# Four gathers by depth for each unit of index keys, a tile of its own for block B's keys, and a bit loop of four operations with a slot each

## The chip, the cores and the metric

The kernel runs on one core of a Trainium2 chip. The core has a matrix engine (PE, with its weight load shown apart as PEld), a vector engine (DVE), a scalar engine (ACT) and a general engine (POOL); SP issues most DMA transfers. Each engine works through its own list of instructions in a fixed order and stops at the first one whose inputs, or whose output buffer, are not ready. The metric is the device time of one execution in microseconds (us): lower is better.

## The reference, cut to what matters

The computation is one layer of a decoder for a prompt of 1024 tokens and 8 sequences that each decode 4 tokens over 8192 cached ones.

```python
p = split_proj(rmsnorm(x, norm_in) @ w_in)            # 2048 -> 7760 columns
# sparse attention: an indexer scores every earlier token
ki_past = cache_kidx[page_table].reshape(Bd, past, IDX_DIM)      # 8 x 8192 x 64
ki_all  = jnp.concatenate([ki_past, ki_new], axis=1)
dots = jnp.einsum("bthd,bld->bthl", qi, ki_all)                  # 16 heads x 64
s    = jnp.einsum("bth,bthl->btl", wi, jax.nn.relu(dots))
_, idx = lax.top_k(s, 256)                # 256 kept for each of 8 x 4 queries
phys = page_table[idx // 128]; off = idx % 128
# attention over the gathered rows cache_k[phys, off], cache_v[phys, off]
conv = short_conv(c * h, state, w_conv)                          # width 3
mix  = concat([attn * silu(z_a), b * conv * silu(z_c)])
y    = x + mix @ w_out
```

The prompt goes through the same layer, with its own keys in place of the cache. A page holds 128 tokens.

## The kernel before

**Main stream.** The projections run in two blocks: block A is the first 512 prompt tokens with the 32 decode tokens (matmuls of 288 and 256 columns), block B the last 512 prompt tokens (512 columns). Every product is three matmuls of high and low parts (`pj`, L512). A weight tile `w` comes in over SP's queue, ACT makes its high part `wh` (L494) and DVE its low part `wl`; `w` has 4 buffers, `wl` and `wh` have 3. The order is: block A's indexer queries, `ki`, heads, gates, convolution; then block B's `ki_tile`, `qi_tiles`, `head_tiles(1)`, gates and eight convolution tiles; then `out_proj0` (block A's output, matmuls of `mx` tiles) and `out_proj1`.

**Slots.** After each chunk of four k-tiles (12 matmuls of 512 columns in block B, 24 of 288 and 256 in block A) the code calls `slot()`. In it four "pipes" of generators each go on to their next `yield`: the main pipe (prompt indexer, decode indexer `keys(g, s)`, prompt attention), the `dec` pipe (decode attention, 4 slots of 11), one for the norm, and the vector pipe (selection of the 256 best: `decode_select` calls `decode_find`). A scheduler then sets every engine's order; the slots decide what is near what.

**Decode indexer.** For each of 8 groups of pages and 8 sequences, `keys(g, s)` gathers 128 rows of 2 KB (8 tokens of 64 values) into `G`, transposes it in four PE instructions into the PSUM tile `gt`, makes `gkh` and `gkl` from that, and multiplies (`gd`, `da`). That makes 64 units.

**Decode selection.** `decode_find` ends a search for the threshold, counts with `tot`, gets the shift `doff`, and then packs the kept positions to the left with eight rounds over 2304 int16 values in `S` (one for each bit of the shift). `way` and `ids` turn that into row numbers, PE sums them (`pidx`) and `rid` is the list for the gathers of decode attention. `kt1`, block B's keys, takes over the buffer of `S` (tag "sc").

**Block B's heads.** A projected key tile goes `kraw`, `p` (PE transposes), `kt` and an inverse square root in small steps `kv`, `krh`, `kr`, `krt` on DVE, then `kp` (PE); the indexer's key does the same as `kit` and `kip`.

**End of decode attention.** The outputs `dpo`, `dos`, `dfin` are gated (`dz`) and stored as `doh` and `dol` by 16 small DMAs; only then is "datt" done. Ahead of block B's last convolution tile stands

```python
    while not need <= done:      # "datt" and "at0" to "at3"
        slot()
    conv_tiles(1, 7, x, lambda ch: load_mix(0, range(4 * ch, 4 * ch + 4), x0))
```

`load_mix` issues the 32 loads of the `mxh` and `mxl` tiles (16 k-tiles, high and low), which hold what was stored.

Of the kernel before, what the change touches and what calls it, by code (L numbers as in the profile page):

```python
# [60 lines left out]
def constants():  # L61
    res, dec = Cst(), Cst()
    res.add("ident", np.eye(128))
    r = np.arange(128)
    res.add("tri", np.concatenate([np.zeros((128, 128)), np.where(r[None, :] <= r[:, None], 0.0, NEG)], 1))
    pos_dec = 8192 + np.arange(32) % 4
    rope = np.zeros((128, 9, 48), np.float32)
    for gi in range(9):
        if gi == 4:
            pos = np.concatenate([np.arange(96), pos_dec])  # L70
        else:
            pos = np.arange(128) + 128 * (gi if gi < 4 else gi - 1)
        c, s = _angles(pos, 16)
        rope[:, gi, 0:16], rope[:, gi, 16:32] = c, s
        c, s = _angles(pos, 8)
        rope[:, gi, 32:40], rope[:, gi, 40:48] = c, s
    res.add("rope", rope.reshape(128, -1))
    c, s = _angles(pos_dec, 16)
    res.add("roped", np.concatenate([c, s], 1))
    q = np.arange(32)  # L80
    res.add("newm", np.where(np.arange(4)[None, :] <= (q % 4)[:, None], 0.0, SENT))
    res.add("own", (q[:, None] // 4 == q[None, :] // 4))
    res.add("prow", (r % 16)[:, None])
    wm = np.zeros((128, 8, 2, 32), np.float32)
    for p in range(128):
        for s in range(8):
            wm[p, s, p // 64, s * 4 + (p % 64) // 16] = 1.0
    dec.add("sel8", (np.arange(8)[:, None] == r[None, :] // 16))
    e16 = np.zeros((32, 2, 128), np.float32)
    for qq in range(32):  # L90
        e16[qq, qq // 16, (qq % 16) * 8:(qq % 16) * 8 + 8] = 1.0
    dec.add("e16", e16.reshape(32, -1))
    same = r[:, None] % 32 == r[None, :] % 32
    dec.add("msum", same)
    dec.add("mlow", same & (r[:, None] < r[None, :]))
    selk, selv = np.zeros((128, 132)), np.zeros((128, 2, 32))
    for p in range(128):
        selk[p, p // 8 * 8 + 4 + p % 4] = 1.0
        selv[p, p // 8 % 2, p // 16 * 4 + p % 4] = 1.0
    dec.add("selk", selk)  # L100
    dec.add("selv", selv.reshape(128, -1))
    dec.add("iota", np.broadcast_to(np.arange(256) - 256, (128, 256)))
    dec.add("wmask", wm.reshape(128, -1))
    cq = np.zeros((2, 128, 800), np.float32)
    tok = np.concatenate([np.arange(256, 512), pos_dec, np.arange(512, 1024)])
    c, s = _angles(tok, 8)
    cq[0] = 1.0
    for h in range(2):
        cq[0, h * 64:h * 64 + 8], cq[0, h * 64 + 8:h * 64 + 16] = c.T, c.T
        cq[1, h * 64:h * 64 + 8], cq[1, h * 64 + 8:h * 64 + 16] = -s.T, s.T  # L110
    return res, dec, cq


def build(tc, ctx, I, O, stop=None):
# [40 lines left out]
    def sm(shape, dt=F32, name="sm"):  # L155
        n = int(np.prod(shape[1:]))
        return sp.tile(list(shape), dt, tag="s" if n > 16 else "t", bufs=6 if n > 16 else 16, name=name)
# [4 lines left out]
    def psb(shape=(128, 512), name="psb"):  # L162
        return pp.tile(list(shape), F32, tag="b", bufs=3, name=name)
# [6 lines left out]
    def const(shape, name, dt=F32):  # L170
        return cp.tile(list(shape), dt, name=name, tag=name)
# [64 lines left out]
    def cs(name, rows=128):  # L236
        a, n = res.cols[name]
        return cst[:rows, a - 128:a - 128 + n]
# [38 lines left out]


    hp = [0]
    CY, OS = 1, 2  # L280
    waiting, pipes, later = object(), [], []

    def front(f):
# [201 lines left out]
    def load_w(view, eng=None):  # L485

        m = view.shape[-1]
        with first() if eng is None else nullcontext():
            w = wp.tile([128, 4, 128], F32, tag="w", bufs=4, name="w")
            lo = wp.tile([128, 4, 128], F32R, tag="wl", bufs=3, name="wl")  # L490
            hi = wp.tile([128, 4, 128], F32R, tag="wh", bufs=3, name="wh")
            w, lo, hi = w[:, :, :m], lo[:, :, :m], hi[:, :, :m]
            nc.sync.dma_start(w, view)
            nc.scalar.copy(hi, w)  # L494
            (tt if eng is None else eng.tensor_tensor)(lo, w, hi, SUB)
        return hi, lo
# [214 lines left out]

    def head_tiles(b, x):
        if b == 1:
            while "dsel" not in done:
                slot()
            kt1 = gp.tile([128, 2, 2, 512], F32R, tag="sc", bufs=1, name="kt1")
            kth[1], ktl[1] = kt1[:, 0], kt1[:, 1]
        for kv in range(2):
            follow(k_rest(b, kv, proj1(w_in, C_K + 128 * kv, 128, x, HALVES[b])))
            slot()  # L720
        for kv in range(2):
            follow(v_rest(b, kv, proj1(w_in, C_V + 128 * kv, 128, x, HALVES[b])))
            slot()
        for h in range(8):
            follow(q_rest(b, h, proj1(w_in, C_Q + 128 * h, 128, x, HALVES[b])))
            slot()
        follow(q_norm(b))
# [308 lines left out]
    def decode_index():  # L1036
        while not {"qi0", "ki0"} <= done:
            yield waiting
        st, acc = {}, {}
        cki = I["cache_kidx"].rearrange("o n (r e) d -> (o n r) (e d)", e=8)  # L1040
        zq = lambda z, s: z[:, s].rearrange("p r t h -> p (r t h)")
        keep = dec_c.cols["iota"][0]
        dc = const((128, keep), "dc")
        dcs = lambda k, r=128: dc[:r, dec_c.cols[k][0]:dec_c.cols[k][0] + dec_c.cols[k][1]]
        idx = const((128, 64), "gidx", I32)
        sc["msum"], sc["mlow"] = dcs("msum"), dcs("mlow")
        sc["e16"] = dcs("e16", 32).rearrange("q (g p) -> q g p", g=2)
        sc["selk"], sc["selv"] = dcs("selk"), dcs("selv").rearrange("p (k c) -> p k c", k=2)

        def tables():  # L1050
            nc.sync.dma_start(dc, I["dcst"][:, :keep])
            pt8i, pt8 = sm((8, 64), I32, name="pt8i"), sm((8, 64), name="pt8")
            nc.sync.dma_start(pt8i.rearrange("j (s g) -> j s g", s=8), I["page_table"].rearrange("s (g j) -> j s g", j=8))
            nc.vector.tensor_copy(pt8, pt8i)
            pp8 = psb((128, 64), name="pp8")
            nc.tensor.matmul(pp8, dcs("sel8", 8), pt8, start=True, stop=True)
            ts(idx, pp8, 16.0, cs("prow"), MUL, ADD)
            st["idx"] = idx
            yield 1

# [31 lines left out]
        def keys(g, s):  # L1092
            while "idx" not in st:
                yield 1
            G = g2((128, 512), name="G")
            nc.gpsimd.indirect_dma_start(out=G, out_offset=None, in_=cki,  # L1096
                                         in_offset=bass.IndirectOffsetOnAxis(ap=idx[:, 8 * s + g:8 * s + g + 1], axis=0))
            yield 1
            yield 1
            pt = psb((128, 512), name="gt")  # L1100
            for e in range(4):
                transpose(pt[:, 128 * e:128 * e + 128], G[:, 128 * e:128 * e + 128])
            kh, kl = g2((128, 512), F32R, name="gkh"), g2((128, 512), F32R, name="gkl")
            nc.scalar.copy(kh, pt)
            tt(kl, pt, kh, SUB)
            yield 1
            while "z" not in st:
                yield 1
# [11 lines left out]
            if s == 7:  # L1120
                c = g // 2
                tmp = g2((64, 512), name="stmp")
                nc.scalar.copy(tmp, acc[0][64:128])
                dst = sc["S"][32 * c:32 * c + 32, (g % 2) * 1024:(g % 2) * 1024 + 1024].rearrange(
                    "q (p e r) -> q r e p", e=4, r=2)
                for r in range(2):
                    rs = slice(32 * r, 32 * r + 32)
                    tt(dst[:, r], acc[0][rs].rearrange("q (e p) -> q e p", e=4),
                       tmp[rs].rearrange("q (e p) -> q e p", e=4), ADD)
# [36 lines left out]
    def decode_find():  # L1166
# [54 lines left out]
        for j in range(2):  # L1221
            xj = x[:, 256 + 1024 * j:1280 + 1024 * j]
            stt(xj, mv[:, half[j]], off, eq[j], ADD, MUL)
            ts(xj, xj, -1.0, None, MUL)
            yield 1
        for b in range(8):
            ts(mv, x, 1 << b, None, ALU.bitwise_and)
            ts(mv, mv, 0.0, -1.0, ALU.is_gt, MUL)
            tt(mv, mv, x, ALU.bitwise_and)
            for _ in range(CY):  # L1230
                yield 1
            tt(x, x, mv, ALU.bitwise_xor)
            tt(x[:, :2304 - (1 << b)], x[:, :2304 - (1 << b)], mv[:, 1 << b:], ALU.bitwise_or)
            for _ in range(CY):
                yield 1
        way, ids = g2((128, 256), name="way"), g2((128, 256), name="ids")
        pg, of = (g2((128, 256), I32, name=f"pg{j}") for j in range(2))
        ac, tmp = (g2((128, 256), I16, name=f"pt{j}") for j in range(2))
# [13 lines left out]
        for j in range(1, 16):  # L1252
            ts(tmp, pg, float(j), ptc[:, j:j + 1], ALU.is_equal, MUL)
            tt(ac, ac, tmp, ADD)
            if j % 4 == 3:
                yield 1
        stt(ids, ac, 128.0, of, MUL, ADD)
        stt(ids, way, 0.5, ids, ALU.is_ge, MUL)
# [290 lines left out]
    x = x1  # L1549
# [69 lines left out]
```

## Time and profile before

| | |
|---|---|
| time, median of 3 runs | 2208.34 us (2207.94 to 2208.93) |
| the profiled execution | 2209.53 us |
| its span on the core | 2207.6 us, mean granted clock 0.995 |
| PE busy | 2162.5 us (98%) |
| PEld busy | 1941.8 us (88%) |
| DVE busy | 1317.3 us (60%) |
| ACT busy | 1088.3 us (49%) |
| POOL busy | 480.5 us (22%) |

The span is what the profiler saw between the first and the last instruction; 1.9 us of the execution lie around it. Busy shares are means over stages, so a stage is read from its own rows.

### The profile page before, as it was taken

Reading aid. Unit: us, or ns where it says so; the run is one execution under the profiler, and the core shown is the slowest. Engines: PE = TensorE matmul, PEld = TensorE weight load, DVE = VectorE, ACT = ScalarE, POOL = GpSimd, SP = SyncE. Lnnn points to the kernel's source line nnn. Section 1 sums busy time; section 2 is a strip of 40 time slices with the busy share of each in tenths; the row PEclk is TensorE's granted clock in tenths of the full one; section 3 lists DMA queues with packets and bytes.
Section 4 is the critical chain, followed back from the end, with each engine's and each line's share of the span. In section 5 each row is a group of like instructions: output and inputs, shape, how many; then the busy total and the mean of one; then the engine's idle time right before and its main releaser. Section 6 shows DMA issues by size and latency. Waiting matters only on the chain.

```text
span 2207.6 us, 37829 instructions
## 1 busy us (share of the span) xinstructions
PE 2162.5 (98%) x13502; PEld 1941.8 (88%) x13502; DVE 1317.3 (60%) x2994; ACT 1088.3 (49%) x2112; POOL 480.5 (22%) x697
## 2 busy tenths in 40 slices
PE   6999999999999999999899999999999999999999
PEld 5899999999999999787688888888888899999887
DVE  6556666555555654799866666556667556443222
ACT  4346666334436566422257684445675565332221
POOL 2111011111113222142531143432331111210000
PEclk9999999999999999999999999999999999999999
DMA  5423444344344333333343344433343384448343
GB/s 195 131 90 117 125 138 135 118 141 131 123 144 140 118 116 104 107 117 113 102 134 117 117 150 129 118 122 105 113 128 113 102 301 117 123 119 275 134 134 110
DMA packets 203720, 290.81 MB, mean 132 GB/s; under 512 B 37588, under 2 KB 87948, under 8 KB 203404
## 3 DMA queue, kind: packets, MB, share of 16 engines
q1 hardware_dynamic: 192268, 254.83, 36.0%
q0 software_dynamic: 11264, 33.57, 5.5%
q8 instruction: 106, 1.74, 0.3%
q14 instruction: 82, 0.67, 0.1%
HBM read 247.53 MB, written 40.78 MB: 131 GB/s over the span
## 4 chain that ended last, share of the span: by engine, by line
PE 50%; DMA 0%; DVE 0%; issue 0%; POOL 0%
PE pj L512 33%; PE po L1503 8%; PE ix L855 1%; PE ix L854 1%; PE pt L174 1%; PE lg L1346 1%; PE dpo L1412 1%; PE kst L174 1%; PE sc L178 1%; PE sc L179 1%; PE po L179 1%; PE po L177 1%; PE po L178 1%; PE sc L177 1%; PE p L174 0%; PE pq L174 0%
## 5 line engine op out<-in xcount | busy, mean ns | idle before, releaser
L512 PE MATMUL pj<-xh,wl 128*128 128x288 f32 (+2 forms) x2800 | 793.0, 329 | 6.9 <-DVE wl L121 6.8
L512 PE MATMUL pj<-xh,wh 128*128 128x288 f32 (+2 forms) x2800 | 791.1, 328 | 6.9 <-DVE xl L121 2.7
L512 PE MATMUL pj<-xl,wh 128*128 128x288 f32 (+2 forms) x2800 | 796.1, 330 | 0.0
L121 DVE TENSOR_TENSOR wl<-w,wh 128x512 fp32r<-128x512 f32 (+1 forms) x613 | 444.1, 726 | 431.2 <-ACT wh L494 397.2
L494 ACT CAST wh<-w 128x512 fp32r<-128x512 f32 x616 | 379.2, 616 | 604.8 <-PE pj L512 380.0
L512 PEld LDWEIGHTS pj<-xh,wh 128*128 128x128 f32 (+1 forms) x2800 | 477.1, 189 | 51.8 <-DVE xl L121 3.1
L512 PEld LDWEIGHTS pj<-xh,wl 128*128 128x128 f32 (+1 forms) x2800 | 474.6, 189 | 51.6 <-DVE wl L121 11.2
L512 PEld LDWEIGHTS pj<-xl,wh 128*128 128x128 f32 (+1 forms) x2800 | 475.1, 189 | 42.2
L886 ACT ACTIVATE junk<-acc,se,se 128x512 int8<-128x512 f32 (+5 forms) x186 | 181.1, 974 | 27.4 <-DVE se L121 24.2
L1096 POOL DMA_INDIRECT G<-in_cache_kidx,gidx x64 | 64.3, 1004 | 388.6 <-PE gd L179 140.4
L121 DVE SCALAR_TENSOR_TENSOR acc<-ixr,wsg,acc 128x512 f32<-128x512 f32 (+3 forms) x150 | 98.3, 668 | 45.9 <-ACT ixr L857 44.7
L857 ACT ACTIVATE ixr<-ix,wab 128x512 f32<-128x512 f32 (+3 forms) x160 | 95.3, 613 | 54.9 <-PE ix L855 53.6
L512 PE MATMUL pj<-mxh,wl 128*128 128x272 f32 x512 | 109.8, 292 | 0.0
L512 PE MATMUL pj<-mxl,wh 128*128 128x272 f32 x512 | 109.4, 291 | 0.0
L512 PE MATMUL pj<-mxh,wh 128*128 128x272 f32 x512 | 108.9, 291 | 0.0
L1392 POOL DMA_INDIRECT Vs<-in_cache_v,rid x64 | 66.4, 1038 | 123.8 <-DVE Vl L121 36.1
L1004 ACT CAST pthl<-pt 128x256 fp32r<-128x256 f32 x144 | 49.6, 371 | 80.6 <-PE pt L174 79.4
L121 DVE TENSOR_TENSOR pthl<-pt,pthl 128x256 fp32r<-128x256 f32 x144 | 57.2, 420 | 50.6 <-ACT pthl L1004 50.0
L512 PEld LDWEIGHTS pj<-mxh,wh 128*128 128x128 f32 x512 | 81.5, 189 | 0.7
L512 PEld LDWEIGHTS pj<-mxl,wh 128*128 128x128 f32 x512 | 81.6, 189 | 0.3
L512 PEld LDWEIGHTS pj<-mxh,wl 128*128 128x128 f32 x512 | 81.3, 189 | 0.4
L990 POOL TENSOR_SCALAR P<-P,l 128x128 f32<-128x128 f32 (+7 forms) x64 | 51.9, 811 | 133.5 <-DVE l L989 102.7
(430 smaller groups left out, 3233.7 us busy)
## 6 DMA issues: line engine op xcount, KB each, us to landing
w<-in_w_in SPq DMA_DIRECT2D x480, 256.0 KB
w<-in_w_out SPq DMA_DIRECT2D x128, 256.0 KB
q_d<-qt SPq DMA_DIRECT2D x72, 64.0 KB
xr<-in_x_a SPq DMA_DIRECT2D x16, 272.0 KB
out_y_a<-xr SPq DMA_DIRECT2D x16, 272.0 KB
xq<-in_x_prompt SPq DMA_DIRECT2D x8, 512.0 KB
xq<-in_x_prompt SPq DMA_DIRECT2D x16, 256.0 KB
q<-q_d SPq DMA_DIRECT2D x32, 128.0 KB
```

The lines of the kernel that those rows point to most:

```text
L121: i = f(*a, **k)
L174: nc.tensor.transpose(out, in_, ident[:p, :p])
L177: nc.tensor.matmul(out, lh, rh, start=start, stop=False)
L494: nc.scalar.copy(hi, w)
L512: nc.tensor.matmul(p[:m, :n], w[c][:, k % 4], x[k][b][:, a:a + n], start=(k == 0 and c == b), stop=(k == KT - 1 and c == 1))
L857: nc.scalar.activation(out=r[:, :w], in_=ps[:, :w], func=AF.Relu, scale=wab[:, g, h:h + 1])
L886: nc.scalar.activation(out=junk[:, :n], in_=S, func=AF.Sign, scale=sg, bias=cand, accum_out=s)
L990: nc.gpsimd.tensor_scalar(P[:, :n], P[:, :n], l, 0.5, MUL, MUL)
L1004: nc.scalar.copy(t[:, 0], ptv)
L1096: nc.gpsimd.indirect_dma_start(out=G, out_offset=None, in_=cki, in_offset=bass.IndirectOffsetOnAxis(ap=idx[:, 8 * s + g:8 * s + g + 1], ax ...
L1392: nc.gpsimd.indirect_dma_start(out=W[:, hf], out_offset=None, in_=cv, in_offset=bass.IndirectOffsetOnAxis(ap=rid[:, hf, q:q + 1], axis=0))
L1503: nc.tensor.matmul(ps[i], x[k_][b][:, 128 * i:128 * i + 128], w[c], start=(k_ == 0 and c == b), stop=(k_ == KT - 1 and c == 1))
```

## The change

- `cache_kidx` is laid out on the host by depth, and `keys` does four gathers of 128 rows of 512 bytes into `G`, which then holds what `gt` held: the four transposes and `gt` go. The index table grows from 128x64 to 128x8x8x4.
- `kt1` becomes a constant tile, and the loop that waited for "dsel" ahead of it goes.
- In the bit loop `ts` and `tt` become one `scalar_tensor_tensor`, and each of the four operations is followed by a `yield` (before: two `yield`s in five operations). Two more `yield`s stand in the loop ahead, and four more in the loop over pages. Decode selection thus takes 22 slots more.
- `wl` and `wh` get a fourth buffer. The scratch area of the software DMA descriptors is set to 2048 bytes.

```diff
-            lo = wp.tile([128, 4, 128], F32R, tag="wl", bufs=3, name="wl")
-            hi = wp.tile([128, 4, 128], F32R, tag="wh", bufs=3, name="wh")
+            lo = wp.tile([128, 4, 128], F32R, tag="wl", bufs=4, name="wl")
+            hi = wp.tile([128, 4, 128], F32R, tag="wh", bufs=4, name="wh")
...
         if b == 1:
-            while "dsel" not in done:
-                slot()
-            kt1 = gp.tile([128, 2, 2, 512], F32R, tag="sc", bufs=1, name="kt1")
+            kt1 = const((128, 2, 2, 512), "kt1", F32R)
...
-            G = g2((128, 512), name="G")
-            nc.gpsimd.indirect_dma_start(out=G, out_offset=None, in_=cki,
-                                         in_offset=bass.IndirectOffsetOnAxis(ap=idx[:, 8 * s + g:8 * s + g + 1], axis=0))
-            yield 1
-            yield 1
-            pt = psb((128, 512), name="gt")
+            G = g2((128, 4, 128), name="G")
             for e in range(4):
-                transpose(pt[:, 128 * e:128 * e + 128], G[:, 128 * e:128 * e + 128])
+                nc.gpsimd.indirect_dma_start(out=G[:, e], out_offset=None, in_=cki,
+                                             in_offset=bass.IndirectOffsetOnAxis(ap=idx[:, s, g, e:e + 1], axis=0))
+            yield 1
+            yield 1
+            G = G.rearrange("p e t -> p (e t)")
             kh, kl = g2((128, 512), F32R, name="gkh"), g2((128, 512), F32R, name="gkl")
-            nc.scalar.copy(kh, pt)
-            tt(kl, pt, kh, SUB)
+            nc.scalar.copy(kh, G)
+            tt(kl, G, kh, SUB)
...
             ts(mv, x, 1 << b, None, ALU.bitwise_and)
-            ts(mv, mv, 0.0, -1.0, ALU.is_gt, MUL)
-            tt(mv, mv, x, ALU.bitwise_and)
-            for _ in range(CY):
-                yield 1
+            yield 1
+            stt(mv, mv, 0.0, x, ALU.is_gt, MUL)
+            yield 1
             tt(x, x, mv, ALU.bitwise_xor)
+            yield 1
             tt(x[:, :2304 - (1 << b)], x[:, :2304 - (1 << b)], mv[:, 1 << b:], ALU.bitwise_or)
-            for _ in range(CY):
-                yield 1
+            yield 1
...
-            if j % 4 == 3:
+            if j % 2 == 1:
                 yield 1
...
-    nc = _bacc.Bacc("TRN2", target_bir_lowering=False, num_devices=1)
+    nc = _bacc.Bacc("TRN2", target_bir_lowering=False, num_devices=1, dynamic_dma_scratch_size=2048)
```

Three places show what this does to the engines' orders.

**PE, end of the selection.** Before, `pidx` of the decode selection stands among block B's `pj` (its two `kp` come 27 rows ahead of it and 24 behind it):

```order
L512 MATMUL pj<-xl,wh 128x512
L512 MATMUL pj<-xh,wl 128x512
L512 MATMUL pj<-xh,wh 128x512
L1263 MATMUL pidx<-dc,ids 128x32 x2
L174 MATMUL pqd<-ident,qd_12690 128x32 x8
```

With the change the same place reads:

```order
L512 MATMUL pj<-xl,wh 128x512
L512 MATMUL pj<-xh,wl 128x512
L174 MATMUL kp<-ident,kt 128x128 x4
L1260 MATMUL pidx<-dc,ids 128x32 x2
L174 MATMUL p_13445<-ident,vraw 128x128 x4
```

Counted in `pj` matmuls from the program's start, `tot` moved from 5705 to 5945 and `pidx` from 6121 to 6144, so between them stand 199 where 416 stood; the first `kip` of block B moved from 5971 to 6048 and its last `kp` from 6143 to 6144. The decode indexer's last `gd` moved from 3761 to 4122, its first from 1685 to 1680.

**DVE, same stretch.** Before, the steps of a key tile's inverse square root (`kv`, `krh`, `kr`) stand around the last operations on `S`:

```order
L639 TENSOR_REDUCE kv<-ksq 128x4
L121 TENSOR_TENSOR S<-S 128x2304
L121 TENSOR_TENSOR wl<-w,wh 128x512
L121 TENSOR_SCALAR kv<-kv 128x4
L121 TENSOR_TENSOR S<-S 128x2176
L121 TENSOR_SCALAR krh<-kv 128x4
L121 TENSOR_TENSOR wl<-w,wh 128x512
L1239 TENSOR_REDUCE way<-S 128x256
```

With the change they stand between the operations of earlier bits:

```order
L121 TENSOR_TENSOR S<-S 128x2272
L121 TENSOR_TENSOR krt<-kr 128x4
L121 TENSOR_TENSOR wl<-w,wh 128x512
L121 TENSOR_SCALAR S<-S 128x2304
L121 SCALAR_TENSOR_TENSOR krt<-krt,kv 128x4
L121 SCALAR_TENSOR_TENSOR S<-S 128x2304
L121 SCALAR_TENSOR_TENSOR kr<-krt,kr 128x4
L121 TENSOR_TENSOR S<-S 128x2304
L121 TENSOR_TENSOR krt<-kr 128x4
L121 TENSOR_TENSOR S<-S 128x2240
```

From `doff` to `ids` DVE has 164 instructions in place of 192: `wl` stands there 16 times instead of 33, the 5 `qish` and 5 `qit` are gone, `S` has 8 operations fewer, and 7 small ones of a second `kr` are new.

**SP, end of decode attention.** Before, weight loads and others stand between the stores of `doh` and `dol` and the loads of `mxh` and `mxl`:

```order
L1438 DMA mx_7h<-doh 128x16
L1439 DMA mx_7l<-dol 128x16
L493 DMA w<-in_w_in 128x512
L748 DMA mx_14h<-mh 128x512
L493 DMA w<-in_w_in 128x512
L749 DMA mx_14l<-cm 128x512
```

With the change the loads follow at once, and the next weight tile comes behind all 32:

```order
L1435 DMA mx_7h<-doh 128x16
L1436 DMA mx_7l<-dol 128x16
L1453 DMA mxh<-mx_0h 128x544
L1453 DMA mxl<-mx_0l 128x544
L1453 DMA mxh<-mx_1h 128x544
```

On PE the last `dfin` moved from `pj` number 8191 to 8400, which is the last one of the input projections: behind it 113 matmuls follow without a `pj` (42 `po`, 24 `pt`, 24 `sc`, the rest `dpo`, `dfin` and others; 85 of them up to the last `dfin`), and then `out_proj0`. On ACT 9 search steps (`junk`), 10 `pthl` and 11 other operations stand between that last `pj` and `doh`. The loop that waits for "datt" ran no slot before and runs 15 with the change.

## Rows read from the trace of the kernel before

**Rows 1.** The page: busy time of PE and its share of the span.

```profile
PE 2162.5 (98%) x13502; PEld 1941.8 (88%) x13502; DVE 1317.3 (60%) x2994; ACT 1088.3 (49%) x2112; POOL 480.5 (22%) x697
```

**Rows 2.** PE's waits: what for, total us, times, longest.

```profile
PE p L174 <- DVE kt L121: 3.0, 1, 3.0
PE kp L174 <- POOL kt L551: 1.8, 1, 1.8
```

**Rows 3.** PE's timeline around one unit's transposes: start us, duration us, instruction, count.

```profile
277.64 0.41 PE L512 MATMUL pj<-xh,wl 128*128 128x288 f32 x2
277.89 0.60 PE L174 MATMUL gt<-ident,G 128*128 128x128 f32 x4
278.25 0.50 PE L512 MATMUL pj<-xh,wh 128*128 128x288 f32 x2
278.59 0.41 PE L512 MATMUL pj<-xl,wh 128*128 128x288 f32 x2
```

**Rows 4.** The tile gt: durations ns min/median/max, first and last start.

```profile
L174 PE MATMUL gt<-ident,G x256: 269/272/273, 277.9 to 637.3; 128*128 128x128 f32 x128
```

**Rows 5.** The tile Ks (decode attention's key gathers), and POOL's idle time before them.

```profile
L1321 POOL DMA_INDIRECT Ks<-in_cache_k,rid x64: 942/950/1549, 1092.9 to 1493.2; - x64
...
  issue: 14.5, 45
```

**Rows 6.** POOL's timeline at the first gathers of G.

```profile
266.66 1.15 POOL L1096 DMA_INDIRECT G<-in_cache_kidx,gidx  x1 [92.76 <-DMA wmask<-in_dcst]
268.12 1.20 POOL L1096 DMA_INDIRECT G<-in_cache_kidx,gidx  x1 [0.30 <-issue]
```

**Rows 7.** DMA issues: count, median us from issue to landing.

```profile
G<-in_cache_kidx,gidx POOLq DMA_INDIRECT x64, 3.6
```

**Rows 8.** Window from doff to ids: length, busy us of each engine, granted clock, DMA.

```profile
969.30:1086.20 116.90, 104.48 (x461) 82.11 (x461) 116.01 (x198) 29.19 (x55) 43.57 (x38) 0.96 0.32 103
```

**Rows 9.** DVE's groups by form, 900 to 1100 us: busy us, mean ns.

```profile
L121 DVE TENSOR_TENSOR wl<-w,wh 128x512 fp32r<-128x512 f32 x55 | 45.7, 832 | 13.5 <-ACT wh L494 13.5
L121 DVE TENSOR_TENSOR S<-S 128x2304 int16<-128x2304 int16 x16 | 25.4, 1589 | 0.0
L121 DVE TENSOR_SCALAR S<-S 128x2304 int16<-128x2304 int16 x16 | 15.8, 986 | 0.1
L622 DVE STREAM_SHUFFLE qish<-pj 128x512 f32<-128x512 f32 x8 | 5.9, 734 | 0.0
L121 DVE TENSOR_TENSOR qit<-pj,cosi 128x512 f32<-128x512 f32 x8 | 5.4, 673 | 0.0
...
L121 DVE SCALAR_TENSOR_TENSOR S<-S,doff,deq 128x1024 int16<-128x1024 int16 x2 | 3.0, 1524 | 0.0
L121 DVE SCALAR_TENSOR_TENSOR deq<-dcs,dkp,deq 128x1024 int16<-128x1024 int16 x2 | 2.5, 1274 | 0.0
```

**Rows 10.** PE's timeline in block B inside that window.

```profile
1039.69 0.39 PE L512 MATMUL pj<-xh,wh 128*128 128x512 f32 x1
1039.92 0.40 PE L512 MATMUL pj<-xl,wh 128*128 128x512 f32 x1
```

**Rows 11.** SP's timeline: first and last store of decode attention's second half.

```profile
1726.10 0.33 SPq L1438 DMA_DIRECT2D mx_0h<-doh  x1
...
1734.00 0.43 SPq L1439 DMA_DIRECT2D mx_7l<-dol  x1
```

**Rows 12.** SP's timeline: first and last of the 32 mx loads.

```profile
1760.81 0.33 SPq L1456 DMA_DIRECT2D mxl<-mx_0l  x1
...
1786.97 0.32 SPq L1456 DMA_DIRECT2D mxh<-mx_15h  x1
1787.60 0.32 SPq L1456 DMA_DIRECT2D mxl<-mx_15l  x1
```

**Rows 13.** The tile mxh: the first matmuls of out_proj0.

```profile
L512 PE MATMUL pj<-mxh,wh x512: 283/288/374, 1782.2 to 2026.0; 128*128 128x272 f32 x171
```

**Rows 14.** ACT's groups by form, 1690 to 1900 us: busy us, mean ns.

```profile
L886 ACT ACTIVATE junk<-acc,se,se 128x1024 int8<-128x1024 f32 x31 | 38.5, 1241 | 5.7 <-DVE se L121 5.5
...
L1004 ACT CAST pthl<-pt 128x256 fp32r<-128x256 f32 x28 | 9.5, 368 | 13.5 <-PE pt L174 13.3
...
L886 ACT ACTIVATION_READ_ACCUMULATOR junk<-acc,se,se 128x1 f32 x31 | 5.9, 189 | 0.0
```

More of the change, by code (lines that the diff above doesn't have):

```diff
@@ L82, in constants @@
     res.add("own", (q[:, None] // 4 == q[None, :] // 4))
-    res.add("prow", (r % 16)[:, None])
+    res.add("prow", (r % 64)[:, None])
     wm = np.zeros((128, 8, 2, 32), np.float32)
@@ L87, in constants @@
             wm[p, s, p // 64, s * 4 + (p % 64) // 16] = 1.0
-    dec.add("sel8", (np.arange(8)[:, None] == r[None, :] // 16))
+    dec.add("sel2", (np.arange(2)[:, None] == r[None, :] // 64))
     e16 = np.zeros((32, 2, 128), np.float32)
@@ L279, in build @@
     hp = [0]
-    CY, OS = 1, 2
+    OS = 2
     waiting, pipes, later = object(), [], []
@@ L1039, in decode_index @@
         st, acc = {}, {}
-        cki = I["cache_kidx"].rearrange("o n (r e) d -> (o n r) (e d)", e=8)
+        cki = I["cache_kidx"].rearrange("n d t -> (n d) t")
         zq = lambda z, s: z[:, s].rearrange("p r t h -> p (r t h)")
@@ L1044, in decode_index @@
         dcs = lambda k, r=128: dc[:r, dec_c.cols[k][0]:dec_c.cols[k][0] + dec_c.cols[k][1]]
-        idx = const((128, 64), "gidx", I32)
+        idx = const((128, 8, 8, 4), "gidx", I32)
         sc["msum"], sc["mlow"] = dcs("msum"), dcs("mlow")
@@ L1051, in tables @@
             nc.sync.dma_start(dc, I["dcst"][:, :keep])
[L1052 to L1057, printed above, removed]
+            pt2i, pt2 = g2((2, 256), I32, name="pt2i"), g2((2, 256), name="pt2")
+            nc.sync.dma_start(pt2i.rearrange("r (s c) -> r s c", s=8), I["page_table"].rearrange("s (c r) -> r s c", r=2))
+            nc.vector.tensor_copy(pt2, pt2i)
+            pp2 = psb((128, 256), name="pp2")
+            nc.tensor.matmul(pp2, dcs("sel2", 2), pt2, start=True, stop=True)
+            ts(idx.rearrange("p s g e -> p (s g e)"), pp2, 64.0, cs("prow"), MUL, ADD)
             st["idx"] = idx
@@ L1094, in keys @@
                 yield 1
-            G = g2((128, 512), name="G")
-            nc.gpsimd.indirect_dma_start(out=G, out_offset=None, in_=cki,
-                                         in_offset=bass.IndirectOffsetOnAxis(ap=idx[:, 8 * s + g:8 * s + g + 1], axis=0))
+            G = g2((128, 4, 128), name="G")
+            for e in range(4):
+                nc.gpsimd.indirect_dma_start(out=G[:, e], out_offset=None, in_=cki,
+                                             in_offset=bass.IndirectOffsetOnAxis(ap=idx[:, s, g, e:e + 1], axis=0))
             yield 1
             yield 1
-            pt = psb((128, 512), name="gt")
-            for e in range(4):
-                transpose(pt[:, 128 * e:128 * e + 128], G[:, 128 * e:128 * e + 128])
+            G = G.rearrange("p e t -> p (e t)")
             kh, kl = g2((128, 512), F32R, name="gkh"), g2((128, 512), F32R, name="gkl")
-            nc.scalar.copy(kh, pt)
-            tt(kl, pt, kh, SUB)
+            nc.scalar.copy(kh, G)
+            tt(kl, G, kh, SUB)
             yield 1
@@ L1124, in keys @@
                 dst = sc["S"][32 * c:32 * c + 32, (g % 2) * 1024:(g % 2) * 1024 + 1024].rearrange(
-                    "q (p e r) -> q r e p", e=4, r=2)
+                    "q (e r p) -> q r e p", e=4, r=2)
                 for r in range(2):
@@ L1594 @@
     host.update(cst=res.array(), dcst=dec.array(), cq=cq)
+    host["cache_kidx"] = np.ascontiguousarray(host["cache_kidx"][0].transpose(0, 2, 1))
     host["x_a"] = np.ascontiguousarray(np.concatenate([host["x_prompt"][0, :512], host["x_sample"].reshape(32, D)]).T)
```

## The prediction, made before the change was run

> **What bounds the kernel now.** I read the page first: PE is busy 98% of the span [rows 1], so the kernel is its list of matmuls, and a change can shorten that list or make PE wait. Next PE's waits: they are few, and two of them belong to block B's keys, which wait for DVE and POOL at the end of decode selection [rows 2]. Then the stage that the change rewrites: from `doff` to `ids` 116.9 us pass in which DVE is busy 116.0 and PE 104.5 (granted clock 0.96) [rows 8]. DVE is full there, and PE keeps nearly up with it only because 416 `pj` matmuls stand in its list between `tot` and `pidx`. The other place is the passage to `out_proj0`, where PE has no wait: stores end at 1734.4 [rows 11], the loads of what was stored run from 1760.8 to 1787.9 [rows 12], and the first matmul on them starts at 1782.2 [rows 13].
>
> **The transposes that go.** From start to start a pair of `pj` takes 0.25 us, the four `gt` take 0.36, and the pair behind them 0.34 [rows 3]. A unit thus costs 0.36 + 0.09 = 0.45 us, and 64 units (256 transposes [rows 4]) 28.8 us; without the slower pair it is 23.0. I take 28, since the timeline has both pieces. PE has nothing to put in their place, and PE is the bound, so all of it counts.
>
> **The gathers that come.** POOL spends 0.95 us on one and 14.5 / 45 = 0.32 us until the next where nothing holds it [rows 5], so 1.27, and 5.1 us for a unit's four. Before, a unit comes every (637.3 - 277.9) / 63.75 = 5.64 us [rows 4]. The new order puts (4122 - 1680) / 63.75 = 38.3 `pj` into a unit where 32.6 stood, which adds 5.7 x 0.125 = 0.71 [rows 3], and 0.45 goes: 5.9 us. The gathers then hide behind PE, with 0.8 us to spare for each unit. What would end that is a price over 1.48 us. The first two gathers of `G` stand 1.46 us apart [rows 6], and the dearest row is 1.55 us long [rows 5]; with 0.32 behind it that is 1.87, four of them 7.5, and (7.5 - 5.9) x 64 = 102 us. I take nothing, by the 0.95 of the median. Landing takes 3.6 us [rows 7], which two slots and ten buffers cover.
>
> The next gather is issued 1.46 us after the last [rows 6] though each takes 3.6 to land [rows 7], so they overlap. The Trainium skill (DMA: Bandwidth & Descriptors, Anatomy of one DMA) speaks against splitting: it fits a gather from POOL as 2.0 us plus bytes over 436 GB/s, most of it paid per transfer. By that, with transfers in a row, four of 64 KB are an estimated 8.6 us in a unit, 2.7 more than it has, and the kernel would lose about 170 us more; the overlap in the rows says that this is not how it goes.
>
> **The selection.** In a bit, a `TENSOR_SCALAR` of 0.99 and a `TENSOR_TENSOR` of 1.59 us go [rows 9], 2.58 together. The operation in their place has no row at 2304 elements. At 1024 the same form took 1.27 and 1.52 us [rows 9], so 2.9 to 3.4 at 2304; the lower bound is the `TENSOR_TENSOR`'s 1.59. I take 3.15, the middle of its own form, so it saves nothing: +0.57 in each of 8 bits, +4.6 us. Out of the stretch go 17 `wl` (14.1), 5 `qish` (3.7) and 5 `qit` (3.4) [rows 9], and 7 small steps come in, an estimated 1.5. The chain becomes 116.9 - 14.1 - 7.1 + 4.6 + 1.5 = 102 us, with DVE as full as before.
>
> PE's part of the stretch shrinks much more. Between `tot` and `pidx` stand 199 `pj` in place of 416. At 0.23 us each [rows 10] 217 fewer are 50 us, and of 104.5 us of work [rows 8] 54.5 remain. `pidx` needs `ids`, and on the way `kip`, `p` and `kp` stop PE one by one, since the small steps of the keys stand between long operations on `S`. PE has no other list to turn to. It idles 102 - 54.5 = 47.5 us, where it idles 12.4 now [rows 8]: **+35 us**. Bounds: with the new operation at 1.59 the chain is 89.5 and the loss 22; if the chain gets no shorter than 116.9 it is 50.
>
> The cause is the delay of `tot`: 22 more slots, and gathers that spread the units over more `pj`, have moved it 240 `pj` back, while block B's keys, which no longer wait for "dsel", hardly moved.
>
> **The passage to out_proj0.** Decode attention ends later too. Before, `dfin` was done 57 us before the first `mx` matmul [rows 11, 13]; now it stands behind the last `pj` of the input projections. Call the start of that place t0. ACT has 9 search steps of 1.24 + 0.19, 10 `pthl` of 0.37 and 11 others at no less than that ahead of `doh` [rows 14]: 12.9 + 3.7 + 4.1 = 20.7 us. With the waits for DVE between the steps I take 25. The 16 stores take 8.3 us [rows 11], and behind them stand all 32 loads. These took 27 us with 7 weight loads among them [rows 12], so 32/39 of it, 22; the last needs some 3 more to land. The first column block of `out_proj0` can end at t0 + 58. PE's work until then: 113 matmuls, by 0.09 for a transpose and 0.125 for 256 columns [rows 3] and 0.23 for 512 [rows 10] some 14 us; 96 matmuls of that column block, 12 us; 2 of others. That is 28, so PE idles **30 us**. If ACT is not behind and `doh` is ready at t0 + 12 it is 17; with 30 us and loads at their old rate, 40.
>
> The fourth `wl` and `wh` buffer could shorten some waits in the first microseconds; I count it and the smaller scratch area at nothing, since PE has 2% to give back in all [rows 1].
>
> **Sum.** The profiled execution took 2209.5, 1.2 us above the median of the runs: 2209.5 - 28 + 35 + 30 = 2246.5. As the median it is **2246 us**, 1.7% slower.
>
> **Rivals.** (1) *The passage stays covered*: `doh` comes before t0, by 30 us or more, and the 30 us fall away: 2216. For it speaks that the 35 us PE idles earlier let ACT and the search steps catch up; against it that the stores follow the last `dfin` in the list, and that this stands behind the last `pj`. (2) *It ends on the other side*: the new DVE operation runs as fast as a `TENSOR_TENSOR` and the passage stays covered. Then 2209.5 - 28 + 22 = 2203, and a little less where the long operations run below their mean of 1.59; it decides where both stalls together come under 28 us. The rows of its own form [rows 9] speak against it, and so does the count of `pj`. (3) *POOL becomes the bound*: gathers at over 1.48 us. At 1.6 with the pause the units take 6.4 and the kernel some 32 us more, 2278; at 1.87 it would be 2348. The median row speaks against it. (4) *Gathers follow one another*, each waiting for the landing of the last: 4 x 3.6 = 14.4 us in a unit of 5.9 [rows 7] and 64 x 8.5 = 544 us more, about 2790. The first two gathers [rows 6] speak against it. The Trainium skill's page named above, with its 8.6 us for a unit, would make that about 2420.
>
> **Chances.** Both stalls, 2222 to 2275: 0.60. Rival 1, 2204 to 2222: 0.15. Rival 2: 0.17. Rival 3: 0.06. Rival 4: 0.02. A difference under 0.2% (4.4 us) can't be told from none in this kernel. Rival 2 and the lower edge of rival 1 give faster 0.17 and same 0.06, the rest slower 0.77. To hold 8 in 10 I leave out most of rival 2 and of rivals 3 and 4: 2200 to 2277.
>
> **What would show it.** In the changed kernel's profile: no `gt`; `pj` pairs 0.25 us apart throughout the decode indexer; 256 gathers 1.3 us apart, and PE without waits for `gd`. Between `doff` and `ids` some 102 us, DVE full, PE busy about half, its waits put down to DVE `kt`, `kit` or `ids`. A new operation on `S` near 3 us. Behind the last `pj` of the input projections PE waits for `mxh` and `mxl` by DMA. I am wrong if PE works on through either place: then the list of PE was not what it waits in, or DVE's chain is shorter than its old rows make it; a gap before `gd` would mean that the gathers are dear.

## The result, and the profile after

The change takes **2265.94 us** (median of 4 runs, 2259.22 to 2272.89) against 2208.64 for the kernel before beside it: ratio 1.0258, with a 95% interval of 1.0227 to 1.0290. Run again in a later job (e9 below) it took 2230.63 against 2207.42 there, ratio 1.0118 (1.0097 to 1.0138). It is slower in both; where the two differ is the third of the points below.

The page of the changed kernel, its span, the row that answers to [rows 1], and the granted clock in 40 slices (tenths of TensorE's full clock; before, every slice had a 9). In these traces the clock is recorded as full or half, so a value between is a mean over a stretch with both:

```profile
span 2257.4 us, 37600 instructions
PE 2155.0 (95%) x13246; PEld 1925.7 (85%) x13246; DVE 1315.5 (58%) x2986; ACT 1084.9 (48%) x2112; POOL 682.2 (30%) x889
PEclk9999999999999999998799999999999989999999
```

PE has 256 instructions fewer and is still busy nearly as long, because it ran some of them at the lower clock; the span is 49.8 us longer. The profiled execution is the fastest of the four, so the profile holds 50 of the 57 us between the medians. PE's waits, as in [rows 2], say where (what for, total us, times, longest):

```profile
PE kp L174 <- POOL kt L551: 20.6, 1, 20.6
PE pj L512 <- issue: 14.8, 24, 2.5
PE pt L174 <- POOL P L988: 6.3, 3, 4.7
PE pj L512 <- DMA mxh<-mx_0h: 4.2, 1, 4.2
```

Two are the expected ones: block B's keys, and the loads of `mxh`. The second, 24 short waits for nothing that the profile shows ("issue"), is new.

Where the time goes is best seen by counting PE's `pj` matmuls, which both kernels have in the same number. The table is worked out from the traces: the start of the n-th `pj` in the kernel before, and how much later it starts in five others. A and B are the change in its two profiles, C the gathers alone and D the bit loop alone (experiments e10 and e3 below), E the gathers with three gate tiles moved (e12).

```
 pj     before       A       B       C       D       E
 1600    270.7    -4.1    -6.9     1.1     0.4     0.0   first gathers
 1700    285.4    10.6    -7.8     0.1     0.4    -1.0
 4400    733.4    -8.3   -41.3   -33.9     0.4   -34.6   decode indexer done
 6040   1059.7   -11.7   -45.6   -37.4     0.0   -38.3   selection
 6150   1103.5    26.4    -7.6     0.5     4.6   -54.3
 6300   1154.7    21.6   -12.4     1.3     0.0    13.8
 6800   1298.9    24.1    -9.8     1.3     0.5     3.3
 8400   1781.9    21.5   -12.4     1.3    -1.2     4.9   last pj of w_in
 8401   1782.2    57.4    23.8     1.3    32.5     4.8   first of out_proj0
  end   2207.6    49.8    17.5     1.4    26.7     2.4
```

**The selection.** The window from `doff` to `ids`, as [rows 8] (length, busy PE, PEld, DVE, ACT, POOL, granted clock, DMA), and DVE's operations in it, as [rows 9]:

```profile
1022.40:1124.30 101.90, 65.85 (x267) 51.55 (x266) 98.44 (x165) 19.55 (x39) 41.08 (x36) 0.77 0.20 62
```

```profile
L121 DVE SCALAR_TENSOR_TENSOR S<-S 128x2304 int16<-128x2304 int16 x8 | 21.4, 2678 | 0.0
L121 DVE TENSOR_TENSOR wl<-w,wh 128x512 fp32r<-128x512 f32 x17 | 12.0, 708 | 0.0
L121 DVE TENSOR_TENSOR S<-S 128x2304 int16<-128x2304 int16 x8 | 11.8, 1472 | 0.0
...
L121 DVE TENSOR_SCALAR S<-S 128x2304 int16<-128x2304 int16 x8 | 6.3, 785 | 0.1
...
L121 DVE SCALAR_TENSOR_TENSOR S<-S,doff,deq 128x1024 int16<-128x1024 int16 x2 | 3.1, 1566 | 0.0
```

The chain takes 101.9 us with DVE busy 98.4, and PE, with 267 instructions where 461 stood, idles 36 us of it; its granted clock is 0.77 in the mean of the stretch. The new operation (first row) takes 2.68 us.

**The passage to out_proj0.** SP's rows that answer to [rows 11] and [rows 12] (start us, duration), and the window up to `out_proj0`:

```profile
1828.07 0.32 SPq L1435 DMA_DIRECT2D mx_0h<-doh  x1
...
1836.09 0.44 SPq L1436 DMA_DIRECT2D mx_7l<-dol  x1
1836.57 0.43 SPq L1453 DMA_DIRECT2D mxh<-mx_0h  x1
...
1858.76 0.32 SPq L1453 DMA_DIRECT2D mxl<-mx_15l  x1
```

```profile
1803.50:1839.50 36.00, 21.83 (x119) 17.16 (x117) 21.25 (x78) 31.40 (x62) 6.49 (x13) 0.81 0.43 112
```

The last `pj` of the input projections starts at 1803.5. From there to the first store are 24.6 us, the stores take 8.5 and the loads 22.2. In the 36 us until `out_proj0` begins (the window's row), PE works 21.8 at a mean clock of 0.81 and ACT is busy for 31.4: the search steps and casts ahead of `doh`. Up to the end of `out_proj0`'s first column block, 55.5 us behind that last `pj`, PE works 40.3.

**The first gathers.** The run of gathers starts at 265.5. The window 265 to 290 us of the change in the first profile, and then in the second (e9):

```profile
265.00:290.00 25.00, 15.49 (x90) 13.29 (x89) 8.82 (x27) 10.41 (x25) 15.54 (x16) 0.72 0.38 108
```

```profile
265.00:290.00 25.00, 25.00 (x191) 24.37 (x191) 18.90 (x57) 18.25 (x43) 19.01 (x20) 1.00 0.55 173
```

The same list of instructions: PE starts 90 matmuls in one and 191 in the other. In the first, these rows of the timelines stand there (PE, ACT, DVE, SP, and POOL's steady row; "remote" means that the view names nobody who ended the wait):

```profile
279.93 0.57 PE L512 MATMUL pj<-xl,wh 128*128 128x256 f32 x1 [0.32 <-issue]
280.30 0.72 PE L512 MATMUL pj<-xh,wl 128*128 128x288 f32 x2
282.75 0.40 PE L512 MATMUL pj<-xh,wh 128*128 128x288 f32 x1 [1.73 <-issue]
...
279.96 0.62 ACT L494 CAST wh<-w 128x512 fp32r<-128x512 f32 x1 [9.03 <-remote]
...
282.85 0.69 DVE L121 TENSOR_TENSOR wl<-w,wh 128x512 fp32r<-128x512 f32 x1 [11.47 <-remote]
...
270.69 13.21 SPq L493 DMA_DIRECT2D w<-in_w_in  x2
...
277.04 0.95 POOL L1095 DMA_INDIRECT G<-in_cache_kidx,gidx  x1 [0.30 <-issue]
```

While POOL issues a gather each 1.25 us, PE moves on in small steps, and ACT, DVE and SP's weight loads stand still. It is PE that is late, and the others wait for it: the semaphore that ACT's cast and DVE's `wl` wait for is one that PE's matmuls raise (the trace has it rise at 279.94 and 282.75), and SP's second load goes out at 283.57, as soon as that `wl` is done. PE's own idle times there end with no signal that the profile shows. What held it isn't in the trace.

### The profile page after: what moved, and what is told of

The parts are those of the page before. It is cut to its first block, busy times and chain, and to the rows that moved or that the text cites. A ratio compares the mean times of both kernels' runs of the same rounds, so it can differ in the third digit from the quotient of the medians.

```text
span 2257.4 us, 37600 instructions
## 1 busy us (share of the span) xinstructions
PE 2155.0 (95%) x13246; PEld 1925.7 (85%) x13246; DVE 1315.5 (58%) x2986; ACT 1084.9 (48%) x2112; POOL 682.2 (30%) x889
## 4 chain that ended last, share of the span: by engine, by line
PE 49%; DMA 1%; ACT 1%; SPq 0%; DVE 0%; issue 0%; POOL 0%; ACTq 0%; DVEq 0%
PE pj L512 32%; PE po L1500 8%; PE ix L853 1%; PE ix L852 1%; PE pt L174 1%; PE lg L1343 1%; PE dpo L1409 1%; PE kst L174 1%; PE po L177 1%; PE po L178 1%; PE po L179 0%; PE sc L179 0%; PE sc L178 0%; PE sc L177 0%; ACT junk L884 0%; DMA q<-q_d 0%
## 5 line engine op out<-in xcount | busy, mean ns | idle before, releaser
L1095 POOL DMA_INDIRECT G<-in_cache_kidx,gidx x256 | 258.5, 1010 | 247.1 <-ACT qsq L637 96.0
L1500 PE MATMUL po<-wh,mx 128*128 128x512 f32 x352 | 108.3, 389 | 0.0
L1015 POOL TENSOR_TENSOR zt<-zt 128x256 fp32r<-128x256 f32 x32 | 27.6, 861 | 205.8 <-ACT zt L1014 205.5
L1318 POOL DMA_INDIRECT Ks<-in_cache_k,rid x64 | 65.9, 1029 | 75.0 <-issue 25.5
```

The source lines that it names most:

```text
L1095: nc.gpsimd.indirect_dma_start(out=G[:, e], out_offset=None, in_=cki, in_offset=bass.IndirectOffsetOnAxis(ap=idx[:, s, g, e:e + 1], axis=0))
L1318: nc.gpsimd.indirect_dma_start(out=K[:, hf], out_offset=None, in_=ck, in_offset=bass.IndirectOffsetOnAxis(ap=rid[:, hf, q:q + 1], axis=0))
L1500: nc.tensor.matmul(ps[i], x[k_][b][:, 128 * i:128 * i + 128], w[c], start=(k_ == 0 and c == b), stop=(k_ == KT - 1 and c == 1))
```

## The experiments

**e1, e2: the gathers alone.** The kernel before, with the host's layout, the index table and this, with the small scratch area (e1) or the default one (e2):

```diff
-            G = g2((128, 512), name="G")
-            nc.gpsimd.indirect_dma_start(out=G, ...)
+            G = g2((128, 4, 128), name="G")
+            for e in range(4):
+                nc.gpsimd.indirect_dma_start(out=G[:, e], ...)
...
-            for e in range(4):
-                transpose(pt[:, 128 * e:128 * e + 128], G[:, 128 * e:128 * e + 128])
```

> The kernel before with the four gathers in place of the transposes and the small scratch area, and nothing else: kt1 in the buffer of S, two slots and five operations a bit, three buffers of wl and wh. In PE's list tot stands at pj 5944 and pidx at 6122, and the last dfin at 8191, as before. Theory (the gathers alone push tot back and open the wait in the selection; the slots alone open the passage to out_proj0; the first burst of gathers costs PE some 14 us): -28 for the transposes, +31 in the selection, +14 at the first gathers, nothing at the passage: about 2226. Rival A (the passage opens with the late decode selection, whatever the slots): 2256. Rival B (the wait in the selection belongs to the slots or to kt1): 2195.

> The same with the descriptor scratch at its default size. The lists of all engines are the same. Theory (the waits of PE, ACT and DVE at the first gathers come from 16 gathers in a row): as the kernel with the small scratch, about 2226, and waits between 270 and 290 us in both. Rival (the small scratch makes them): 14 us less, about 2212, and no waits there.

e1 took 2244.26 us, ratio 1.0155 (1.0138 to 1.0172), e2 2239.26, ratio 1.0138 (1.0121 to 1.0154). Both show the waits at the first gathers, so the small scratch does not make them; the 5 us between the two are less than the 14 over which the four runs of the change spread. The passage to `out_proj0` stays covered, and the selection loses 38 us in e1 between `pj` 6040 and 6150: the gathers alone open that wait. They came out 18 and 13 us over the number expected: e1 stands at -0.2 at `pj` 4400, where the sum had -14, so the gathers cost PE more than the waits that I had counted, and the selection took 38 where the sum had 31.

**e3: the bit loop alone.** The kernel before with the four operations, a slot behind each, and the other new slots:

```diff
             ts(mv, x, 1 << b, None, ALU.bitwise_and)
-            ts(mv, mv, 0.0, -1.0, ALU.is_gt, MUL)
-            tt(mv, mv, x, ALU.bitwise_and)
+            yield 1
+            stt(mv, mv, 0.0, x, ALU.is_gt, MUL)
+            yield 1
```

> The kernel before with the bit loop and the slots of the change alone: one gather a unit and the transposes stay. tot stands at pj 5705 and pidx at 6124, as before, the last dfin at 8400. Theory: the selection loses some 5 us (a bit costs DVE 0.4 us more), the passage 30 to 36: about 2246. Rival (the passage opens only with the wait in the selection): about 2210.

2232.34 us, ratio 1.0103 (1.0086 to 1.0120). In the table (D) nothing is lost up to `pj` 8400 (4.6 us in the selection come back by `pj` 6300), 34 us at the first matmul of `out_proj0`, and 27 at the end. The bit loop with its slots opens the passage, without the long wait in the selection. In the window before that first matmul PE works 21.2 of 33.9 us, at a mean clock of 0.84, and the one behind it has 0.80:

```profile
1780.70:1814.60 33.90, 21.23 (x107) 16.65 (x106) 20.02 (x73) 28.28 (x57) 7.70 (x13) 0.84 0.41 112
1814.60:1840.00 25.40, 24.00 (x146) 21.90 (x147) 10.95 (x40) 16.48 (x31) 4.79 (x10) 0.80 1.03 372
```

**e4: the change with the old slots.** All of the change, but each bit yields twice, as before, and the other loops too:

```diff
             ts(mv, x, 1 << b, None, ALU.bitwise_and)
-            yield 1
             stt(mv, mv, 0.0, x, ALU.is_gt, MUL)
             yield 1
             tt(x, x, mv, ALU.bitwise_xor)
-            yield 1
```

> The change with its four operations a bit but the slots of before (two a bit, and those of the other loops). tot stands at 5959, pidx at 6121, the last dfin at 8204. Theory: the passage is covered again, the wait in the selection stays at 30 to 35 and the one at the first gathers at 14: about 2227, 35 to 40 under the change. Rival (the cost of the passage is the gathers' delay): 2260.

2246.15 us, ratio 1.0166 (1.0149 to 1.0183): as e1, and 20 under the change. Its lateness at `pj` 8400 and behind it is the same (36.8), so the passage is covered again, with the new operations in place: what opens it is the slots. It is not as low as expected because the gathers cost PE as much as in e1, and its selection loses 45 us (`pj` 6040 to 6150).

**e5, e6, e7: two remedies.** e5 gives `G` two buffers of its own, so that POOL can't issue far ahead; e6 moves block B's eight gate tiles ahead of its heads, so that PE has other work while DVE goes through the chain; e7 has both. All are built on e1.

```diff
-            G = g2((128, 4, 128), name="G")
+            G = gp.tile([128, 4, 128], F32, tag="G", bufs=2, name="G")
...
+    for h in range(8):
+        z_tile(1, h, x)
+    done.add("z1")
     head_tiles(1, x)
-    for h in range(8):
-        z_tile(1, h, x)
-    done.add("z1")
```

> The gathers alone (the first experiment), with a tag of its own and two buffers for G in place of a share in ten. The lists of PE and DVE are those of the first experiment. POOL can then issue 8 gathers ahead at most. Theory (PE, ACT, DVE and SP are held up once some seven gathers follow each other without a pause; runs of 4 cost nothing): the waits without a visible releaser between 270 and 290 us go, some 15 us and part of the 9 us behind it: about 2226. Rival A (each of 256 gathers costs its share, bunched or not): stays at 2244. Rival B (two buffers make PE wait for gd): above 2250.

> The gathers alone (the first experiment), with block B's eight gate tiles (z_tile) projected ahead of its heads. tot stands at pj 5944 as there, pidx at 6370 in place of 6122, the keys' kp at 6480 and 6527: 426 pj stand between tot and pidx. Theory (PE idles in the selection for want of other work in its list while DVE works through the chain): the 38 us lost there go, about 2208, with the waits at the first gathers left. Rival (what PE does meanwhile slows the chain, or the keys stop PE later): 2230 and over.

> Both edits: two buffers for G and the gates ahead of the heads, on the gathers alone. Theory: the costs are apart and both go: 2244 - 18 - 36 = 2190, faster than the kernel before by 0.9%. Rival: one of them comes back elsewhere, 2205 and over.

They took 2205.03, 2208.67 and 2208.69 us, ratios 0.9990 (0.9980 to 0.9999), 0.9997 (0.9988 to 1.0007) and 1.0000 (0.9990 to 1.0009). Taken by their numbers, e5 and e6 each seem to cure something, and e7's rival held. The traces say otherwise: PE has no wait in the decode indexer in any of the three, and e6, without the two buffers, issues 40 gathers in a row with PE busy for all of the 50 us:

```profile
265.00:315.00 50.00, 50.00 (x376) 48.55 (x376) 34.71 (x108) 36.32 (x84) 37.99 (x38) 1.00 0.52 157
```

These ran on another chip than e1 to e4. The theory that long runs of gathers hold up the others has fallen as it stood, and with it the reading of e5.

**e8: the change with the gates first**, in the same job.

> The whole change, with the gates ahead of the heads. pidx moves from pj 6144 to 6426 while tot stays at 5945; the last dfin stays behind the last pj of the input projections (8400). Theory: the selection's 37 us go, the passage to out_proj0 keeps its 30, the first gathers their 15: about 2229. Rival (the passage is late because the selection stalled, and closes with it): about 2200.

2231.62 us, ratio 1.0102 (1.0086 to 1.0119). The number fits, the reason does not: on that chip the waits at the gathers are missing, which gives some 30 us, and the gates gave nothing, as e9 shows, the change without them on a chip without those waits.

**e9, e10, e11: the change, the gathers alone and e5 once more, side by side on a third chip.**

> The change as it is, beside the next two on one chip. In the profile of the change and of the first, second and fourth experiment PE, ACT, DVE and SP were held up by 17 to 21 us within the gathers; in the fifth to eighth, on another chip, by nothing, even in runs of 20 and 40 gathers, so the theory of long runs has fallen as it was put. Theory now (it belongs to the chip or the run, not to the kernel): here all three kernels show the waits, at 2266, 2244 and 2242, or none does, at 2235, 2207 and 2205. Rival (two buffers for G take it away): the change 2266, the gathers alone 2244, with two buffers 2205.

> The gathers alone once more, the same kernel as in the first experiment. Theory (chip or run): as the change here, either with the waits at 2244 or without them at about 2207. Rival: 2244 in any case.

> The gathers alone with two buffers for G once more. Theory (chip or run): with the waits, if the two others have them, at about 2240, without them at 2205. Rival (two buffers take the waits away): 2205 in any case, while the gathers alone stand at 2244.

2230.63, 2206.15 and 2204.97 us, ratios 1.0118 (1.0097 to 1.0138), 0.9998 (0.9988 to 1.0008) and 0.9989 (0.9980 to 0.9999). The change lost 35 us of its time and the gathers alone 38, with nothing edited, while the kernel before took 2209.44, 2207.77 and 2207.42 in the three jobs. Two buffers for `G` are worth 1 us at most, which is within the spread. So the waits at the gathers belong to the chip or the job, and only kernels with four gathers a unit show them: the kernel before and e3 have none in the job that has them. (On which chip the result itself ran isn't on record.) The DMA view of the two profiles of the change, 274 to 284 us (queues with packets, MB, share), shows that in the first no packet of SP's queue moved for 10 us. It had none to move: its last packets were done at 273.5, and SP sent no load between 271.0 and 283.57, waiting for DVE, and so for PE:

```profile
DMA packets 261, 0.55 MB, mean 55 GB/s; under 512 B 127, under 2 KB 127, under 8 KB 261
q0 software_dynamic: 261, 0.55, 21.2%
```

```profile
DMA packets 1397, 1.65 MB, mean 165 GB/s; under 512 B 244, under 2 KB 884, under 8 KB 1395
q1 hardware_dynamic: 1152, 1.11, 36.8%
q0 software_dynamic: 243, 0.52, 17.4%
q14 instruction: 2, 0.02, 1.0%
```

**e12: three gates first**, on two buffers for `G`: the edit of e6 with `range(3)` ahead of the heads and `range(3, 8)` behind.

> Two buffers for G, and three of block B's eight gate tiles ahead of its heads. tot stands at pj 5944, pidx at 6264 (320 between, 178 without the gates ahead), the keys' kp at 6240 and 6288, the last dfin at 8138. With all eight ahead the selection's wait went, but PE lost as much later, where decode attention, the indexer and block B's keys stood in its list without a pj among them. Theory (three tiles fill the selection and leave the others for what follows): 33 us less than without them, about 2172 on a chip without the waits. Rival (that loss comes with any gate ahead): 2205.

2208.05 us, ratio 1.0000 (0.9990 to 1.0009). The rival held. PE comes to the selection 38.3 us ahead of the kernel before and is 54.3 ahead behind it (E), but by `pj` 6800 all of that is given back. Its windows from the keys' steps on:

```profile
1040.00:1096.00 56.00, 39.16 (x157) 30.41 (x156) 54.10 (x100) 10.55 (x18) 19.04 (x17) 0.83 0.23 73
1096.00:1170.00 74.00, 62.22 (x298) 48.16 (x297) 49.76 (x111) 45.10 (x95) 46.75 (x60) 0.85 0.34 100
```

In the second, decode attention and the indexer stand in PE's list without a `pj` between them, and it stops for about a microsecond at a time:

```profile
1144.80 0.29 PE L1345 MATMUL lg<-ksh,zk 128*48 128x256 f32 x1 [0.89 <-ACT ksh L1334]
1145.62 0.32 PE L1345 MATMUL lg<-ksl,zk 128*48 128x256 f32 x1 [0.54 <-DVE ksl L121]
...
1147.43 0.50 PE L854 MATMUL ix<-kih,qie 128*128 128x512 f32 x1 [1.26 <-DVE qie L121]
```

It idles 12 us in these 74, and its mean clock is 0.85, which on 62 us of work is an estimated 9 us more. From `pj` 6040 to 6800 PE idles 28.6 us here and 38.8 with the gathers alone (e10): the wait has shrunk by 10 and moved, and the stretch takes 281 and 278 us.

## Why the prediction was right, and where it was not

**The direction and the range held; the median came out 20 us over the forecast in the result and 15 under it in e9.** The two stalls that made it slower are there, at the places named.

**The transposes: 28 expected, 29.9 measured where nothing disturbs.** From `pj` 1600 to 4400 PE has no wait in the kernel before nor in e10, and the stretch takes 462.6 and 427.7 us. Added up by instruction, from start to start, 22.7 of these 34.9 us are the 256 `gt`, and 7.2 are the same 2800 `pj`, which pass faster without them: 0.47 us for a unit, against the 0.45 of the one unit that I read. The other 5.0 are 59 matmuls of the prompt's attention and selection, which the new order puts behind `pj` 4400; they are moved and not saved. In the first profile 4 us are left of it all (A, -4.1 to -8.3).

**The gathers: nothing expected; in the first profile this is the step that failed.** The price was right: 0.95 us and 0.30 to the next, in every profile, and POOL never became the bound. On the two chips of e5 to e12 PE has no such wait in the decode indexer, as forecast. In the first profile, and in e1, e2 and e4, the inference failed that a gather that POOL can issue in time costs nobody else. PE took 458.5 us from `pj` 1600 to 4400 where e10 took 427.7: 31 us, of which it idled 19.4, and the rest lies in slower matmuls. The first 14.7 fall within 100 `pj` (A, -4.1 to 10.6). No row of POOL shows it, and ACT, DVE and SP follow PE in it. The kernel before never issued more than three gathers of `G` in a row, so no row there could have shown it. The Trainium skill (DMA: Bandwidth & Descriptors, Anatomy of one DMA) fits one such DMA as 2.0 us plus bytes over 436 GB/s. The estimate from it, 8.6 us for a unit's four in a row, isn't borne out: they are issued 1.25 us apart (the row of POOL above), four in 5.0 us, and e10 comes out at 2206.

**The selection: 35 expected, 38 measured between `pj` 6040 and 6150 in either profile of the change (33 by 6300).** The chain came out at 101.9 us against the 102 of the sum. Two of its parts were off against each other: the new operation took 2.68 and not 3.15, which gives 3.8 us back, and the rest of the stretch took that much more than my sum, by subtraction. The Trainium skill (Vector Engine (DVE) Microarchitecture Reference, Points that are easy to get wrong) says that this form halves its throughput with two sources in SBUF that are not bf16. The rows agree roughly, if the `TENSOR_TENSOR` of that size is the measure: 2.68 against 1.47. The idle time was forecast as 47.5 and is 36, since PE's work in the window took 66 us in place of 54.5. Some 5 of these 11 are my count: I took 217 matmuls out, the `pj` between `tot` and `pidx`, and from `doff` to `ids` 194 are gone. The rest lies in the lower clock, which the sum had left out. As the chain sets the end, the loss is the same.

The cause was named half wrong. I gave both the slots and the gathers; the slots come behind `tot` and can't have delayed it. e10 has the loss with the old slots (38 us); e3, with the new ones, has 4.6 us, and nothing by `pj` 6300. It is the gathers: with them alone `tot` comes 239 `pj` later, since the order spaces their units wider.

**The passage: 30 expected, 30 and 28 measured** (B, -12.4 to 17.5; A, 21.5 to 49.8). Term by term: `doh` 24.3 us behind t0 against 25, stores 8.5 against 8.3, loads 22 against 22, end of the first column block at t0 + 55 against 58. The idle time in it is half of the forecast, 15 us (40.3 of 55.5 worked) and not 30: the work that I had put at 28 us took 40, at a mean clock of 0.82. Here too the end is set by others, so the loss comes out the same. That the 22 slots do it is shown by e3, which has them with the new bit loop and nothing else, and by e4, which has all but them.

**The sum.** In medians, the gathers alone give -1.3 on the third chip (e10) and the bit loop +22.9 on its own (e3); together 21.6 of the 23.2 us that the change costs in e9. `kt1`'s own tile, the fourth buffers and the scratch area have 2 us between them, within the spread of the runs. In the profile of e9 the change costs 17.5, 19.5 less than the sum's +37: 6.9 lie ahead of the first gathers, where two profiles of one kernel differ by 5 (e1 -3.9, e10 1.1), and 10.7 more than the 28 were gained from there to `pj` 6040, of which some 5 are waits of PE that the kernel before has there (8.0 us between `pj` 4400 and 6040, 3.1 in e9). The sum's last step was also 1 us off: 2246.5 less the 1.2 is 2245.

**Rivals.** Rival 3 suspected the gathers, but by a higher price that would make POOL the bound; in the first profile they cost PE 31 us at the price of the median row. Rivals 1 and 2 did not come: `doh` lay 24 us behind t0, and the new operation took 2.68 us. Nor did rival 4: gathers are issued 1.25 us apart.

**Open.** Why PE is held up in two jobs while POOL issues gathers, and not in two others on other chips, I can't say: the chip of e1 to e4 wasn't used again, the chip of the result isn't on record, and no run in those jobs kept the gathers apart from each other. Open too is what would recover the 38 us of the selection. More `pj` between `tot` and `pidx` removed the wait and not the loss.

## What to carry to other kernels

Removing work from the bound engine is worth only what the order of all engines leaves of it: here some 30 us of transposes were spent on a selection whose input came 239 matmuls too late. When slots or unit prices change, count in the order how much of the bound engine's work still stands between a long chain's first input and its output, and how far its last output has moved against the first reader behind a queue. And before an experiment is believed, run its base beside it on the same chip: two remedies here seemed to give 39 and 36 us, and gave nothing beyond the spread of the runs.

## What the hardware showed that I had not expected

- With four gathers a unit, PE lost some 30 us in the decode indexer in the job of the result and in that of e1 to e4, and nothing in two others on two other chips, at equal instruction lists. Where it happened, PE's waits of the kind "issue" in the first profile began 7 us and more into runs of 8 or 16 gathers 1.25 us apart, or shortly behind them; behind a run of four there was one, of 0.3 us. In other jobs a run of 40 left PE fully busy.
- A `SCALAR_TENSOR_TENSOR` over 2304 int16 took 2.68 us, 1.16 ns for an element, against 1.57 us for 1024 (1.53 ns) in the same stretch.
- Stretches in which PE waits again and again had a mean granted clock of 0.71 (e10, 1030 to 1110 us) to 0.85 (e12), and matmuls between the waits were slower: 0.40 us for a `pj` of 288 columns at 282.75 us of the first profile, against 0.29 at 272.33, before the clock fell.
